# Alternating softmax and stick-breaking head groups, with two groups' attention in progress at once

## The chip, the cores and the metric

The kernel runs on one core of one Trainium2 chip. The metric is the time of one execution on the device, in microseconds: 2751.64 us, the median of three runs (2748.37 to 2760.12). The core's engines are TensorE (PE), VectorE (DVE), ScalarE (ACT), GpSimd (POOL) and SyncE (SP, which issues most DMAs). Each works through its own instructions in a fixed order; semaphores make one engine wait for another.

## What is computed

One layer of a residual block over 2048 positions of width 1024. The mixer has two kinds of attention side by side, then an output projection and a SwiGLU feed-forward:

```python
u    = rms_norm(h, norm1_w)
proj = u @ w_in                       # [dq | dk | dv | sq | sk | sv]
# softmax kind: 4 heads, two maps per head (q and k normed)
logits = q @ k.T * scale + bias[t5_bucket]      # chunk-causal mask
p      = softmax(logits)
y_diff = rms_norm((p[:, :, 0] - lam * p[:, :, 1]) @ v)
# stick-breaking kind: 8 heads, strictly causal, no softmax
z    = q @ k.T * scale
rem  = reverse_cumsum(log_sigmoid(-z)) - log_sigmoid(-z)
y_sb = rms_norm(exp(log_sigmoid(z) + rem) @ v)
h    = h + concat(y_diff, y_sb) @ w_out
u2   = rms_norm(h, norm2_w)
h    = h + (silu(u2 @ w_gate) * (u2 @ w_up)) @ w_down
```

All products keep close to float32 accuracy by splitting each operand into a high and a low fp16 part and adding three products.

## The kernel before, in words

**Groups.** The columns of `w_in` are cut into eight groups of 384 columns: groups 0 to 3 are one softmax head each (two maps of 64, values of 128), groups 4 to 7 are two stick-breaking heads each. For each group there is a projection (`proj`, 16 row tiles of 128 positions) and an attention (`diff_attn` or `sb_attn`, 16 query rows of 128).

**Softmax row** (`probs`). PE writes scores into PSUM (`sc`, up to 512 keys at a time). DVE copies each chunk to an SBUF buffer z with scale, bias and a running maximum (lines 483 and 487). DVE reduces the maxima into `ng` (line 492), ACT turns them into a bias (493) and takes Exp over the row with sums (497), at most four pieces: two maps by two blocks of 1024 keys. DVE then reduces the sums (500), takes a reciprocal and a factor (502, 503) and combines the two maps (507).

**Stick-breaking step** (`stage_a`), one head and one block of up to 1024 keys. For each chunk PE writes scores, ACT takes two sigmoids (554 into the buffer, 555 in place), DVE runs a scan along the keys (557) and a product (558).

**Values.** Either result is split into fp16 parts: a cast (line 89 on ACT or 93 on POOL) and a subtraction (98, mostly POOL). A transposing DMA turns it into `aT`, and PE multiplies with v into a PSUM buffer `yp` (458). After four rows (two rows in the last group) `finish` norms and splits the output: squares on ACT (416 or 418), a power on POOL (428 or 151), a product on DVE (429), transposes on PE, and the split into `mo` (435, 436), which goes to DRAM.

**Buffers.** The score buffers z (tag `z4`) are nine for both kinds: a softmax row beyond 1024 keys holds four, a stick-breaking step two. `sc` has four PSUM buffers, `yp` two, `aT` five, the fp16 split three.

**Order.** Groups are emitted one after another: 0 to 3, then 4 to 7. The projection runs half a group or more ahead (`advance`). A scheduler at build time then sets every engine's order from what is emitted, by priority, when operands and buffers are ready; the functions marked `pri("at")` have a priority of their own. In `sb_attn` a step's value products are put off by PD = 5 steps (`pend`), in `diff_attn` by one row.

**End of attention.** During the last half of group 7, output-projection rows (`out_proj`, line 761, evictions 764) are emitted between its steps as they become ready; `post` norms and splits each row for the feed-forward, which starts when the rest is done.

Of the kernel before, what the change touches and what calls it, by code (L numbers as in the profile page):

```python
# [11 lines left out]
F32 = mybir.dt.float32  # L12
# [26 lines left out]
QB, KB, ZB, AB, SB, PD = 4, 7, 9, 5, 3, 5  # L39
# [20 lines left out]
def block(tc, a, out):  # L60
# [3 lines left out]
    with top:  # L64
# [186 lines left out]
        with ExitStack() as ph1:  # L251
# [96 lines left out]
            def proj_batch(g, G, B):  # L348
# [3 lines left out]
                if g < 4:  # L352
                    rq = raw[:].rearrange("p t (c e) -> p t c e", e=64)
                    sq = st[:].rearrange("p c t s e -> p (c t s e)")[:, :2048].bitcast(F32)
# [24 lines left out]
            def proj(g, G, fresh=None):  # L379
                for t in range(NT):  # L380
# [6 lines left out]
                    if t % 4 == 0:  # L387
                        st = pp.tile([P, 6, 4, 2, 64], F16, tag="st", name=nm("st"))
                        v = sp.tile([P, 4, 256], F16, tag="v", bufs=KB, name=nm("v"))
                        raw = pp.tile([P, 4, 256], F32, tag="raw", name=nm("raw")) if g < 4 else None  # L390
# [68 lines left out]

            def diff_attn(g, G):  # L460
# [54 lines left out]
                def values(i, aTs, ssum):  # L515
                    r, k = fq(g, i)
                    if r == 0:
                        ypd[0] = ps.tile([P, 512], F32, tag="yp", name=nm("yp"))
                    yp = ypd[0]
                    for q, (b, n, aT) in enumerate(aTs):  # L520
                        pv(G, yp, P * r, aT, b, n, 0, 128, r == 0 and q == 0, r == k - 1 and q == len(aTs) - 1)
                    if r == k - 1:
                        finish(g, G, i, k, yp, ssum)

                prev = None
                for i in range(NT):
                    if i % 4 == 0:
                        level()
                    z = probs(i)
                    if prev is not None:  # L530
                        values(*prev)
                    yield ((i + 1) * (i + 2) / 2 + CD * (i + 1)) / (136 + 16 * CD), i + 1
                    prev = (i, z, sums[0])
                values(*prev)

            def sb_attn(g, G):
# [38 lines left out]
                pend = []  # L575
# [12 lines left out]
                for u in pend:  # L588
                    stage_b(*u)

# [101 lines left out]
            def proj_stream():  # L692
                for g in range(NG):
                    for t, _ in enumerate(proj(g, Gs[g], fresh if g == 0 else None)):
                        if g == 0 and t == 0:
                            build_bias()
                        if g == NG - 1 and t in WT:
                            if t == WT[0]:
                                rp2.extend(norm_gain(a["norm2_w"], w2))
                            load_wo(WT.index(t))  # L700
                        if t == PF and g + 1 < NG:
                            Gs[g + 1] = load_w(g + 1)
# [41 lines left out]
            def out_proj():  # L744
                for t in range(NT):
# [5 lines left out]
                    else:  # L751
                        xf = pp.tile([P, 6, 4, 2, 64], F16, tag="st", name=nm("xf"))[:].rearrange("p c t s e -> p (c t s e)").bitcast(F32)[:, :D]
# [38 lines left out]
            advance(NT - LAG0)  # L791
            for g in range(NG):
                advance(NT * g + 4)
                for fr, i in (diff_attn if g < 4 else sb_attn)(g, Gs[g]):
                    advance(max(NT * g + min(4 * (i // 4 + 1), NT), int(NT * (g + 1 + fr) - (LAG * (1 - LF * fr * (g == NG - 1)) if g else LAG0 + (LAG - LAG0) * fr))))
                    while g == NG - 1 and len(wos) == 4 and outs < Gs[g].get("fin", 0) and (outs + 2) * (outs + 3) / 272 < fr - LO:
                        next(op)
                        outs += 1
            while outs < 12:
# [428 lines left out]
```

## Time and profile before

| | us |
|---|---|
| median of three runs | 2751.64 |
| profiled execution | 2752.86 |
| its span | 2751.1 |
| first softmax Exp / last | 107.3 / 618.3 |
| first stick-breaking sigmoid / last | 612.7 / 1394.1 |
| first output-projection matmul / last | 1216.6 / 1470.9 |
| busy over the span: PE, DVE, POOL, ACT | 2489.3, 1967.9, 1428.8, 1357.8 |

The page's groups name a line of the kernel, an engine, and out<-in by the program's names. Busy time is the time in which at least one of the group's instructions runs; the idle time behind it is what the engine spent just before them, with what ended it. Matmul durations overlap, so the busy time over the count is the better price for one matmul.

### The profile page before, as it was taken

What the parts mean: (1) busy time and instruction counts of PE and PEld (TensorE: products, weight loads), DVE (VectorE), ACT (ScalarE), POOL (GpSimd) and SP (SyncE); (2) the same over time, 40 slices, a digit from 0 to 9 for tenths busy, and PEclk for the clock granted to TensorE, in tenths of its full rate; (3) what the DMA queues carried; (4) which work ended last, traced back from release to release, by engine and by line L of the source; (5) the groups of instructions that cost most, each with busy time, mean ns of one, the idle gap of its engine ahead of it and who ended that gap; (6) DMA issues with size and microseconds to landing.
All of it is one profiled execution on the core that took longest, in us unless ns stands there. A gap on an engine that the chain in (4) does not pass through costs nothing.

```text
span 2751.1 us, 45381 instructions
## 1 busy us (share of the span) xinstructions
PE 2489.3 (90%) x17084; PEld 1411.3 (51%) x17084; DVE 1967.9 (72%) x3752; ACT 1357.8 (49%) x2539; POOL 1428.8 (52%) x1002
## 2 busy tenths in 40 slices
PE   7998989898878786788988899999999999999999
PEld 4655555555545453457775444444444444444444
DVE  6888879797989989977655878777776644443434
ACT  4665656566878778765644535353342211121120
POOL 2567767665454545546655656555654322232322
PEclk9999999999999997989999999999999999999999
DMA  7788787879999988987887665656657845535532
GB/s 231 197 163 182 151 191 160 180 167 206 196 209 194 199 177 150 205 186 202 211 247 271 235 232 192 225 204 213 237 200 280 339 150 187 210 131 199 188 118 93
DMA packets 646829, 543.52 MB, mean 198 GB/s; under 512 B 506368, under 2 KB 573952, under 8 KB 636368
## 3 DMA queue, kind: packets, MB, share of 16 engines
q1 hardware_dynamic: 644784, 538.53, 71.7%
q8 instruction: 134, 2.20, 0.3%
q0 software_dynamic: 512, 1.36, 0.2%
q14 instruction: 87, 0.71, 0.1%
q10 hardware_dynamic: 1312, 0.72, 0.1%
HBM read 261.08 MB, written 147.32 MB: 148 GB/s over the span
## 4 chain that ended last, share of the span: by engine, by line
PE 33%; DVE 7%; DMA 6%; POOL 3%; issue 3%; ACT 2%; SPq 0%; DVEq 0%; POOLq 0%; ACTq 0%
PE pd L1034 12%; PE pm L934 7%; PE pd L934 6%; PE pa L934 5%; DVE wd L215 2%; DMA stages<-in_w_down_dram 1%; DMA aT<-s 1%; POOL stages L98 1%; PE po L761 1%; POOL s L98 1%; DMA X<-xcd 1%; DMA stages<-in_w_up_dram 1%; DVE wu L215 1%; DVE cg L98 1%; DVE cg L999 1%
## 5 line engine op out<-in xcount | busy, mean ns | idle before, releaser
L98 POOL TENSOR_TENSOR s<-z,s 128x1024 f16<-128x1024 f32 (+7 forms) x288 | 473.5, 1652 | 339.3 <-ACT s L89 300.5
L320 PE MATMUL pj<-w,xt 128*128 128x384 f16 x3072 | 574.4, 335 | 28.1 <-DVE st L330 12.6
L320 PEld LDWEIGHTS <-xt 128*128 128x128 f16 x3072 | 300.7, 100 | 239.6 <-issue 39.4
L448 PE MATMUL sc<-kT,qT 128*128 128x512 f16 (+3 forms) x1280 | 346.8, 361 | 72.8 <-DVE z L558 32.1
L557 DVE TENSOR_TENSOR_SCAN z<-z,sc 128x512 f32<-128x512 f32 (+3 forms) x320 | 355.5, 1113 | 70.7 <-ACT sc L555 68.5
L1034 PE MATMUL pd<-wd,act 128*128 128x512 f16 x1764 | 392.9, 380 | 8.5 <-DVE cu L968 7.0
L458 PE MATMUL yp<-v,aT 128*128 128x64 f16 (+1 forms) x4896 | 281.0, 208 | 79.1 <-DMA aT<-s 78.4
L458 PEld LDWEIGHTS <-aT 128*128 128x128 f16 x4896 | 244.9, 102 | 169.1 <-DMA aT<-s 107.7
L934 PEld LDWEIGHTS <-wg 128*128 128x128 f16 x1848 | 181.3, 98 | 224.4 <-issue 10.9
L934 PEld LDWEIGHTS <-wu 128*128 128x128 f16 x1848 | 181.7, 98 | 220.8 <-issue 8.2
L98 POOL TENSOR_TENSOR act<-cg,act 128x512 f16<-128x512 f32 x109 | 150.4, 1390 | 259.4 <-ACT act L993 259.4
L1034 PEld LDWEIGHTS <-act 128*128 128x128 f16 x1764 | 172.8, 98 | 217.0 <-issue 10.9
L89 ACT CAST s<-z 128x384 f16<-128x384 f32 (+7 forms) x216 | 170.5, 790 | 157.8 <-DMA aT<-s 65.4
L98 POOL TENSOR_TENSOR stages<-stages 128x512 f32<-128x512 f32 x97 | 170.2, 1755 | 120.2 <-DVE wg L215 43.2
L98 POOL TENSOR_TENSOR hs<-hs,cu 128x512 f32<-128x512 f32 x102 | 132.6, 1306 | 162.0 <-DVE hs L1040 60.2
L554 ACT ACTIVATE z<-sc,c 128x512 f32<-128x512 f32 (+3 forms) x320 | 203.5, 636 | 10.7 <-PE sc L448 5.9
L558 DVE TENSOR_TENSOR z<-sc,z 128x512 f32<-128x512 f32 (+3 forms) x320 | 193.3, 606 | 8.1
L555 ACT ACTIVATE sc<-sc,c 128x512 f32<-128x512 f32 (+3 forms) x320 | 195.7, 611 | 0.0
L761 PE MATMUL po<-wo,mt 128*128 128x256 f16 x1536 | 182.4, 277 | 11.4 <-DVE xf L764 6.8
L993 ACT CAST act<-cg 128x512 f16<-128x512 f32 x126 | 76.8, 616 | 231.3 <-DVE cg L999 193.4
L1040 DVE SCALAR_TENSOR_TENSOR hs<-pd,c,hs 128x512 f32<-128x512 f32 x144 | 106.2, 747 | 116.8 <-PE pd L1034 104.5
L934 PE MATMUL pm<-X,wu 128*128 128x512 f16 x792 | 179.3, 379 | 1.8 <-ACT cg L979 1.7
(241 smaller groups left out, 4109.9 us busy)
## 6 DMA issues: line engine op xcount, KB each, us to landing
xt<-xs SPq DMA_DIRECT2D x112, 512.0 KB, 4.3
hs<-hd SPq DMA_DIRECT2D x72, 512.0 KB, 4.4
hd<-hs SPq DMA_DIRECT2D x56, 512.0 KB, 6.1
split<-wg SPq DMA_DIRECT2D x11, 1792.0 KB, 6.9
split<-wu SPq DMA_DIRECT2D x11, 1792.0 KB, 6.7
split<-wd SPq DMA_DIRECT2D x11, 1792.0 KB, 6.8
wg<-split SPq DMA_DIRECT2D x11, 1792.0 KB, 7.4
wd<-split SPq DMA_DIRECT2D x11, 1792.0 KB, 9.1
```

Source lines behind the costliest of these rows:

```text
L89: ACT.copy(dst, src)
L98: (DVE if e == "D" else POOL).tensor_tensor(dst, a_, b_, op)
L320: PE.matmul(pj[:, :384], lhsT=xv[:, xi, kt, :], rhs=G["w"][:, wi, kt, :], start=n == 0, stop=n == 23)
L448: PE.matmul(sc[:, : 128 * w].rearrange("p (t n) -> p t n", n=P), lhsT=G["q"][i // 4][:, 2 - 2 * o + m, i % 4, :], rhs=G["k"][q][:, m, 0:w, ...
L458: PE.matmul(yp[:, y0 : y0 + wd], lhsT=aT[:, a_, :], rhs=v[:, v_ : v_ + wd], start=start and j == 0 and q == 0, stop=stop and j == nb - 1 a ...
L554: ACT.activation(om[:, lo:hi], sc[:, :w], AF.Sigmoid, scale=G["nkz"][:])
L555: ACT.activation(sc[:, :w], sc[:, :w], AF.Sigmoid, scale=G["kz"][:])
L557: DVE.tensor_tensor_scan(ov, ov, sc[:, :w], om[:, hi : hi + 1], op0=ALU.mult, op1=ALU.bypass)
L558: DVE.tensor_tensor(be[:, lo:hi], sc[:, :w], om[:, lo + 1 : hi + 1], ALU.mult)
L761: PE.matmul(po[:, sl], lhsT=mt[:, kt, P * xi : P * xi + P], rhs=wos[2 * h + n][wi][:, kt, :], start=q == 0, stop=q == 23)
L934: PE.matmul(ps_[:].rearrange("p (t n) -> p t n", n=P), lhsT=wv[:, wo, wi, 128 * kt : 128 * kt + 128], rhs=X[xo][:, :, xi, kt, :], start=st ...
L1034: PE.matmul(po[:], lhsT=act[:, ao, xi, 128 * j : 128 * j + 128], rhs=W["d"][:, wo, wi, :], start=start and u == 0 and q == 0, stop=u == nu ...
```

## The change

Groups are taken in the order 0, 4, 1, 5, 2, 6, 3, 7, for the projection as for the attention. A driver keeps up to two groups' attention alive. Each has a position: its place in the order plus twice the finished share of its work, so a group spans two units and its neighbour starts when it is half done. The driver always steps the group whose position is lowest. Value products of both kinds go through one list `pend`, put off by PD = 4 units. The projection's pace follows the position. Buffers for kT go from 7 to 8, for v from 7 to 9, and the projection's staging tile `st` shrinks from 6 to 4 parts. The norm2 gain, which lies in the tile of the softmax bias, is fetched once the last softmax group has ended. Output-projection rows start only when group 3 has ended, and a row needs both group 3 and group 7; how many may be out follows a line in the position instead of a square law.

```diff
-QB, KB, ZB, AB, SB, PD = 4, 7, 9, 5, 3, 5
+QB, KB, VB, ZB, AB, SB, PD = 4, 8, 9, 9, 5, 3, 4
+ORDER = (0, 4, 1, 5, 2, 6, 3, 7)
...
+            pend = []
+
+            def push(f):
+                pend.append(f)
+                while len(pend) > PD:
+                    pend.pop(0)()
...
-                    z = probs(i)
-                    if prev is not None:
-                        values(*prev)
+                    aTs = probs(i)
+                    for q, (b, n, aT) in enumerate(aTs):
+                        push(functools.partial(values, i, q, len(aTs), b, n, aT, sums[0]))
...
-                            pend.append((i, m, b, n, aT))
-                            if len(pend) > PD:
-                                stage_b(*pend.pop(0))
+                            push(functools.partial(stage_b, i, m, b, n, aT))
...
-            advance(NT - LAG0)
-            for g in range(NG):
-                advance(NT * g + 4)
-                for fr, i in (diff_attn if g < 4 else sb_attn)(g, Gs[g]):
-                    advance(max(NT * g + min(4 * (i // 4 + 1), NT), int(NT * (g + 1 + fr) - (LAG * (1 - LF * fr * (g == NG - 1)) if g else LAG0 + (LAG - LAG0) * fr))))
-                    while g == NG - 1 and len(wos) == 4 and outs < Gs[g].get("fin", 0) and (outs + 2) * (outs + 3) / 272 < fr - LO:
+            live, nxt = {}, 0
+            while live or nxt < NG:
+                if nxt < NG and all(v >= nxt for v, _ in live.values()):
+                    g = ORDER[nxt]
+                    live[nxt] = (nxt, (diff_attn if g < 4 else sb_attn)(g, Gs[g]))
+                    advance(NT * nxt + 4)
+                    nxt += 1
+                p = min(live, key=lambda k: live[k][0])
+                fr, i = next(live[p][1], (None, None))
+                if fr is None:
+                    del live[p]
+                    if p == NG - 2:
+                        while pend:
+                            pend.pop(0)()
+                        rp2.extend(norm_gain(a["norm2_w"], w2))
+                    continue
+                v = p + 2 * fr
+                live[p] = (v, live[p][1])
+                advance(max(NT * p + min(4 * (i // 4 + 1), NT), int(NT * v + LAG)))
+                if p == NG - 1 and p - 1 not in live and len(wos) == 4:
+                    done = min(Gs[g].get("fin", 0) for g in (3, 7))
+                    while outs < min(done, 12) and (outs + 2) / 14 < v - NG + LO:
                         next(op)
                         outs += 1
```

**The middle of a softmax row.** The row of 1408 keys (pieces of 1024 and 384). Before, on DVE, from the maxima's reduction (L492) to the sums' reduction (L500):

```order
L492 TENSOR_REDUCE ng_5325<-mx_5294 128x2
L503 TENSOR_SCALAR rc_5221<-rc_5221,c_261,sums_5049 128x1
L483 TENSOR_SCALAR z_5458,mx_5457<-sc_5463,c_230 128x512
L426 SCALAR_TENSOR_TENSOR yrs_5135<-yss_5130,er_5136 128x4
L507 SCALAR_TENSOR_TENSOR z_5184<-z_5198,rc_5221,z_5184 128x1024
L507 SCALAR_TENSOR_TENSOR z_5193<-z_5207,rc_5221,z_5193 128x256
L483 TENSOR_SCALAR z_5467,mx_5457<-sc_5468,c_230 128x256
L487 ISA z_5467,mx_5457<-sc_5468,bias,c_230 128x256
L487 ISA mx_5457 128x1
L483 TENSOR_SCALAR z_5473,mx_5457<-sc_5474,c_230 128x512
L429 TENSOR_TENSOR y_5129<-yp_4846,yrs_5135 128x512
L483 TENSOR_SCALAR z_5473,mx_5457<-sc_5478,c_230 128x512
```

The fill is the row before (5184) and the row after (5458); on ACT the bias is followed at once by the four Exps. In the change, DVE has these rows from the reduction (now L500) to the sums (now L508; scan L563, product L564):

```order
L500 TENSOR_REDUCE ng_10294<-mx_10263 128x2
L563 SCALAR_TENSOR_TENSOR z_10417<-z_10417,sc_10419 128x512
L564 TENSOR_TENSOR z_10416<-sc_10419,z_10417 128x512
L563 SCALAR_TENSOR_TENSOR z_10417<-z_10417,sc_10426 128x512
L564 TENSOR_TENSOR z_10416<-sc_10426,z_10417 128x512
L553 COPY z_10463<-z_10186 128x1
L508 TENSOR_REDUCE sums_9667<-s_10297 128x2
L510 RECIPROCAL rc_10303<-sums_9667 128x1
L511 TENSOR_SCALAR rc_10303<-rc_10303,c_261,sums_9667 128x1
```

and ACT has these, from the bias (now L501) on:

```order
L501 ACTIVATE ng_10294<-ng_10294,c_260 128x2
L560 ACTIVATE z_10417<-sc_10426,c_4361 128x512
L561 ACTIVATE sc_10426<-sc_10426,c_4360 128x512
L90 CAST s_10203<-z_10185 128x1024
L505 ACT_TABLE_LOAD
L505 ACTIVATE z_10264,s_10297<-z_10264,ng_10294 128x1024
L505 ACTIVATE z_10273,s_10297<-z_10273,ng_10294 128x384
L505 ACTIVATE z_10279,s_10297<-z_10279,ng_10294 128x1024
L505 ACTIVATE z_10288,s_10297<-z_10288,ng_10294 128x384
L560 ACT_TABLE_LOAD
L560 ACTIVATE z_10463<-sc_10465,c_4361 128x512
```

The neighbouring softmax rows have gone from DVE's fill and stick-breaking work has come; on ACT a chunk's sigmoids, a cast and a table load have come between the bias and the Exps.

**The end of the attention**, on DVE. Before, among the last scans (L557), products (L558) and the output projection's evictions (L764):

```order
L557 SCALAR_TENSOR_TENSOR z_18407<-z_18407,sc_18416 128x512
L545 MEMSET z_18453 128x1
L558 TENSOR_TENSOR z_18406<-sc_18416,z_18407 128x512
L557 SCALAR_TENSOR_TENSOR z_18453<-z_18453,sc_18455 128x512
L98 TENSOR_TENSOR x_18358<-z_18345,x_18358 128x2x512
L764 SCALAR_TENSOR_TENSOR xf_18776<-po_18778,c_14910,xf_18776 128x256
L558 TENSOR_TENSOR z_18452<-sc_18455,z_18453 128x512
L545 MEMSET z_18641 128x1
L557 SCALAR_TENSOR_TENSOR z_18453<-z_18453,sc_18463 128x512
L150 TENSOR_SCALAR xrs_18624<-xss_18622 128x1
L764 SCALAR_TENSOR_TENSOR xf_18776<-po_18829,c_15745,xf_18776 128x256
```

In the change, at the same distance from the end:

```order
L563 SCALAR_TENSOR_TENSOR z_18931<-z_18931,sc_18933 128x512
L564 TENSOR_TENSOR z_18930<-sc_18933,z_18931 128x512
L553 COPY z_18977<-z_18890 128x1
L563 SCALAR_TENSOR_TENSOR z_18931<-z_18931,sc_18940 128x512
L564 TENSOR_TENSOR z_18930<-sc_18940,z_18931 128x512
L563 SCALAR_TENSOR_TENSOR z_18977<-z_18977,sc_18979 128x512
L564 TENSOR_TENSOR z_18976<-sc_18979,z_18977 128x512
L563 SCALAR_TENSOR_TENSOR z_18977<-z_18977,sc_18986 128x512
L551 MEMSET z_19037 128x1
L564 TENSOR_TENSOR z_18976<-sc_18986,z_18977 128x512
```

Scans and products follow each other, and the evictions (now L762) of the output projection stand ahead of all of them or behind.

More of the change, by code (lines that the diff above doesn't have):

```diff
@@ L513, in diff_attn, with values @@
                 ypd = {}
-                def values(i, aTs, ssum):
+                def values(i, q, nq_, b, n, aT, ssum):
                     r, k = fq(g, i)
-                    if r == 0:
+                    if r == 0 and q == 0:
                         ypd[0] = ps.tile([P, 512], F32, tag="yp", name=nm("yp"))
                     yp = ypd[0]
[L520 to L525, printed above, removed]
+                    pv(G, yp, P * r, aT, b, n, 0, 128, r == 0 and q == 0, r == k - 1 and q == nq_ - 1)
+                    if q == nq_ - 1:
+                        if r == k - 1:
+                            finish(g, G, i, k, yp, ssum)
+                            G["fin"] = i + 1
                 for i in range(NT):
```

29 lines of the change are left out of this document (12 added, 17 removed).

## The prediction

> **What bounds the kernel now.** I read the windows of busy time first, to see which engine carries which stretch.
>
> ```profile
> core 0: us, PE busy (x) PEld busy (x) DVE busy (x) ACT busy (x) POOL busy (x), PEclk, DMA share, GB/s
> ...
> 100.00:620.00 520.00, 471.99 (x3734) 302.17 (x3731) 442.79 (x1324) 316.48 (x814) 358.24 (x255) 0.97 0.81 173
> 620.00:1200.00 580.00, 462.83 (x4710) 289.87 (x4709) 514.52 (x919) 449.12 (x868) 300.24 (x194) 0.92 0.95 191
> 100.00:1200.00 1100.00, 934.82 (x8442) 592.04 (x8440) 957.31 (x2242) 765.59 (x1681) 658.48 (x449) 0.94 0.88 183
> 1216.00:1471.00 255.00, 229.52 (x2356) 194.76 (x2355) 168.93 (x273) 135.65 (x215) 152.10 (x101) 0.97 0.85 234
> ...
> 1000.00:1100.00 100.00, 72.48 (x753) 44.38 (x750) 94.41 (x154) 84.37 (x155) 53.12 (x33) 0.83 0.91 170
> ```
>
> From 100 to 620 us the four softmax groups run: PE 472 of 520 (91%), DVE 443 (85%), ACT 316 (61%). From 620 to 1200 us it is the stick-breaking groups: DVE 515 of 580 (89%), ACT 449 (77%), PE 463 (80%). The two kinds lean on different engines, and that is the room the change can use: over the 1100 us the fullest engine is DVE with 957, so 143 us are idle on it. The row of 1000 to 1100 shows that DVE can run at 94%. From 1216 to 1471 us PE leads (230 of 255), because the output projection lies beside the last group. After 1471 us comes the feed-forward, whose code and order the change leaves alone; it only starts earlier or later.
>
> Then the waits of DVE between 100 and 1200 us (total, times, longest), since its idle time is what is for sale.
>
> ```profile
> DVE z L557 <- ACT sc L555: 36.9, 44, 2.9
> DVE z L483 <- PE sc L448: 17.7, 20, 2.1
> DVE y L429 <- POOL yrs L428: 17.7, 7, 5.4
> DVE v L330 <- ACT v L327: 16.5, 12, 3.8
> DVE yrs L426 <- ACT y L416: 8.0, 3, 5.7
> DVE ss L358 <- ACT st L355: 6.6, 6, 2.0
> DVE sums L500 <- ACT z L497: 5.9, 8, 1.6
> DVE mo L436 <- ACT mo L435: 3.6, 3, 2.1
> ```
>
> The seventh row is the one to remember: a softmax row's reduction of the exponentials' sums waited only 5.9 us in all for ACT.
>
> **The change part by part.**
>
> *Amount of work.* The order of instructions has the same matmuls and, within a few rows, the same DVE instructions as before; some 25 casts of the splits move from ACT to POOL. POOL has 1100 - 658 = 442 us idle beside them: no cost. If that cover were gone, a POOL subtraction of 2.2 us (row below) would be late, and the transposed weights behind it.
>
> *Table loads.* ACT now switches between Exp and Sigmoid inside each pair of groups: 97 loads in its order against 5. One costs this:
>
> ```profile
> L554 ACT ACT_TABLE_LOAD x2 | 2.6, 1283 | 0.0
> ...
> 611.43 1.28 ACT L554 ACT_TABLE_LOAD   x1
> 612.72 0.37 ACT L554 ACTIVATE z<-sc,c 128x128 f32<-128x128 f32 x1
> ```
>
> 92 more by 1.283 us are 118 us of ACT. ACT has 1100 - 766 = 334 us idle there and would go to 884 of 1100 (80%), so the sum itself hides. What does not hide is the load that lies in a chain DVE waits for, which is counted next.
>
> *The middle of a softmax row.* DVE reduces the row's maxima (ng), ACT takes the bias and up to four Exp, then DVE needs their sums. While ACT works, DVE lives on what stands in its own order between the two. The durations:
>
> ```profile
> L493 ACT ACTIVATE ng<-ng,c 128x2 f32<-128x2 f32 x56 | 16.4, 294 | 33.8 <-DVE ng L492 33.3
> L497 ACT ACTIVATE z<-z,ng 128x1024 f32<-128x1024 f32 x80 | 91.2, 1140 | 1.3
> L497 ACT ACTIVATE z<-z,ng 128x384 f32<-128x384 f32 x16 | 9.6, 603 | 0.2
> L554 ACT ACTIVATE z<-sc,c 128x512 f32<-128x512 f32 x224 | 157.0, 701 | 5.3 <-PE sc L448 3.6 <-issue 1.6
> L555 ACT ACTIVATE sc<-sc,c 128x512 f32<-128x512 f32 x224 | 151.7, 677 | 0.0
> L89 ACT CAST s<-z 128x1024 f16<-128x1024 f32 x83 | 87.1, 1050 | 77.6 <-issue 16.8 <-DMA xcd<-x 13.8 <-DVE z L558 12.2
> L557 DVE TENSOR_TENSOR_SCAN z<-z,sc 128x512 f32<-128x512 f32 x224 | 285.0, 1272 | 40.1 <-ACT sc L555 39.0 <-PE sc L450 0.4
> L558 DVE TENSOR_TENSOR z<-sc,z 128x512 f32<-128x512 f32 x224 | 153.3, 686 | 5.6
> L547 DVE COPY z<-z 128x1 f32<-128x1 f32 x64 | 9.1, 142 | 0.0
> ```
>
> Take the row of 1408 keys that the change section shows. Before, ACT needs 0.29 + 2 x 1.14 + 2 x 0.60 = 3.8 us, and DVE has about 7.4 us of the neighbouring softmax rows in between. In the change, a chunk's two sigmoids (0.70 + 0.68), a cast (1.05) and a table load (1.28) stand between the bias and the Exps, so ACT needs 7.5 us; DVE has two scans, two products and a copy, 2 x 1.27 + 2 x 0.69 + 0.14 = 4.1 us. DVE falls short by 3.4 us. Counted in the same way, each row of the order by the mean of its shape, over the 56 softmax rows that have such a reduction: before, ACT 3.3 and DVE 5.2 us on average, short in 4 rows, 4 us in all; in the change ACT 5.3 and DVE 4.1, short in 35 rows, 96 us in all. For before the profile has 5.9 us where the count says 4, so I trust the count. Added: 96.4 - 3.9 = **92.5 us**. What is late next is the split of that row (cast, subtraction, transposing DMA) and the next row's evictions, because the nine score buffers z are shared: a late softmax row holds four of them.
>
> The bounds of this term: not below 0, since the waits may fall where PE is the one that is late (PE is 85% busy); not above 92.5 by much, since ACT with 80% load is mostly there when DVE reduces.
>
> *The waits the second group can cover.* Of the quoted waits, those inside a softmax row, a group's finish or the projection's evictions (17.7 + 17.7 + 16.5 + 8.0 + 6.6 + 3.6 = 70.1 us) are answers that take a few us and for which a second stream can supply work. The scan's wait for ACT (36.9) I leave, as ACT gets fuller. Bounds: nothing covered (0), or the whole 143 - 6 = 137. I take **-70.1**.
>
> *The tail.* Output-projection rows now wait until both the last softmax group (3) and the last stick-breaking group (7) have the row, and are then issued in a burst. In DVE's order the last 20 scan chunks stand without a row of the output projection among them; before, they were mixed to the end.
>
> ```profile
> L448 PE MATMUL sc<-kT,qT 128*128 128x512 f16 (+3 forms) x108 | 29.7, 373 | 4.1 <-DVE z L545 1.5 <-DMA qT<-qT 1.2 <-DVE z L547 0.7
> L458 PE MATMUL yp<-v,aT 128*128 128x64 f16 x648 | 28.1, 195 | 11.0 <-DMA aT<-s 11.0
> L98 POOL TENSOR_TENSOR s<-z,s 128x1024 f16<-128x1024 f32 x120 | 263.5, 2199 | 162.6 <-ACT s L89 147.5 <-issue 9.0 <-DMA aT<-s 2.3
> ...
> DMA to landing us min/median/max: 2.3/4.4/7.8
> ```
>
> DVE needs about 38 us for the 20 chunks (1.27 + 0.69 each, two of them smaller). PE has in that place 40 score matmuls at 29.7/108 = 0.28 and 294 value matmuls at 28.1/648 = 0.043, with the mask some 25 us: 13 idle. Behind the last product a cast (1.05), a subtraction (2.2) and a transposing DMA (4.4) stand with nothing beside them: 8 more. **+21 us**; bounds 0 (PE still had stalls of 25 us between 1216 and 1471 that the burst may spare) and 40.
>
> *Edits with one answer.* More buffers for kT and v, a smaller st, one fewer pending unit, the norm2 gain fetched after group 3: no instruction more; SP's number of issues differs by one, and the two kinds' transposes average out DMA shares of 0.81 and 0.95. The gain's DMA goes behind group 3's last use of the bias tile, and only the first output row's normalization could wait for it, by the 4 to 8 us of a DMA landing, hidden under that row's projection.
>
> **Sum**, against the profiled execution's 2752.9 us (1.8 around its span of 2751.1, and 1.2 above the median of 2751.64): 2752.9 + 92.5 - 70.1 + 21 = **2796 us**, 1.6% slower.
>
> **The page on table loads.** The trace's load takes 1.28 us, and the next ACTIVATE starts 0.01 us after it. The Trainium skill, ScalarE: Activation LUTs, section "What ACT_TABLE_LOAD costs", gives about 1283 ns and a drain of about 1380 ns besides, 2.66 us for every switch. By that page 92 switches would be 245 us of ACT, and the 46 new loads ahead of Exps would lengthen the rows' chains by 46 x 1.38 = 63 us, an estimate from the page: 2859. The trace has the page's load but no drain behind it. The same page, section "Table sets: the hidden batching unit", says to group activations by set before switching, which is what the change gives up.
>
> **Rivals.**
>
> *Faster: PE becomes the bound.* DVE's 143 us of idle time could take up the short rows, and with two streams PE would always find a score or a projection to do. At the 91% that it has in the softmax part, 935 us take 1027, DVE then at 957/1027 = 93%, which the row of 1000 to 1100 us shows to be possible: 73 less, 21 more in the tail, 2701. For it: the engines' loads really are complementary. Against: a full DVE leaves no room for 35 short rows.
>
> *No change.* Half of the short rows fall where DVE waited anyway: 2752.9 + 46 - 70 + 21 = 2750.
>
> *Much slower: the shared yp buffers.* Both groups accumulate in one pool of two PSUM buffers, which one group had to itself. A finish holds its buffer through squares, power, product, transposes and the split. The profile's waits of 17.7, 8.0 and 3.6 us lie in it. If each of the 28 finishes between 100 and 1200 us stops the value products for about 3 us, five aT buffers fill and both streams stand: 84 more, 2880. It decides if PE's waits for the finish (yp on mo) exceed those for aT.
>
> *The switch costs more than the load.* If ACT had to empty its pipeline as well, by another 1.28 us, 46 x 1.28 = 59 us would come on top: 2855. The two quoted rows, back to back, speak against it.
>
> That the change doesn't interleave can be left out: the order alternates Exp and Sigmoid 46 times.
>
> **How the numbers follow.** The forecast has 0.45, faster 0.28, no change 0.15, yp 0.09, costlier switches 0.03. The forecast's own range is 2765 to 2850 (tail 0 to 40, covered waits 100 to 30). Reaching toward the faster case and the yp case gives **2690 to 2870** for 8 in 10. A measurement of this kernel tells about 0.5% (14 us) from no change. Faster: 0.28 and a little of the no-change case, 0.30. Same: 0.17. Slower: 0.53.
>
> **What would show it.** Right: DVE's wait at the sums' reduction (5.9 us before) grows to 60 us or more, ACT shows about 97 table loads at 1.28 us without gaps behind them, and DVE's busy share from 100 us to the first output-projection row falls below 87%. The tail: PE idle 20 us more between the first and the last output-projection row. Wrong: if that share rises to 90% or more, the short rows were hidden; if PE's largest wait is yp for mo, the shared buffers decide.

## The result, and the profile after

The changed kernel takes **2989.41 us** (median of four runs, 2978.88 to 2994.32) where the kernel before takes 2750.74 on the same chip: a ratio of 1.0856, 95% interval 1.0817 to 1.0895. It is 239 us slower; 44 were forecast, and the time lies outside the range of 2690 to 2870. The feed-forward from the last output-projection matmul to the end is unchanged: 2989.2 - 1710.5 = 1278.7 us of span after, 2751.1 - 1470.9 = 1280.2 before. All the loss lies ahead of it. The first output-projection matmul starts at 1391.1 instead of 1216.6 us (174.5 later), and the stretch to the last one takes 319.4 instead of 254.3 (65 more).

The line numbers of the attention move by 1 to 8 in the changed kernel: the sums' reduction is 508 (500 before), the scan 563 (557), the eviction of softmax scores 491 (483), of v 331 (330), the value products 459 (458).

Windows of busy time, changed kernel. The first is the stretch from 100 us to the first output-projection matmul, the second the stretch of the output projection, the third 20 us in the middle:

```profile
core 0: us, PE busy (x) PEld busy (x) DVE busy (x) ACT busy (x) POOL busy (x), PEclk, DMA share, GB/s
100.00:1391.00 1291.00, 1002.78 (x8503) 617.14 (x8501) 968.10 (x2236) 869.53 (x1751) 671.06 (x479) 0.89 0.75 161
1391.00:1711.00 320.00, 260.07 (x2527) 211.95 (x2524) 198.27 (x337) 165.58 (x267) 161.18 (x108) 0.89 0.73 199
740.00:760.00 20.00, 16.27 (x160) 10.63 (x157) 3.84 (x14) 6.75 (x23) 10.57 (x9) 1.00 0.83 166
...
0.00:100.00 100.00, 59.25 (x309) 36.63 (x310) 50.21 (x132) 37.30 (x77) 23.61 (x39) 0.83 0.52 163
```

DVE now has 968 of 1291 (75%, 87% before), PE 78% (85%), ACT 67% (70%): no engine became the bound, all three became emptier. Already the first 100 us hold less work: DVE 50 us, 70 in the row of before below. The third row is a seam, where one group ends and the next begins: DVE is busy for 3.8 of 20 us.

The same view, kernel before, for the first stretch:

```profile
0.00:100.00 100.00, 77.65 (x426) 48.63 (x427) 69.88 (x156) 48.03 (x97) 39.27 (x48) 0.97 0.68 218
```

DVE's waits in the changed kernel between 100 and 1450 us (total, times, longest), which answer to the eight rows of the prediction:

```profile
DVE sums L508 <- ACT z L505: 83.2, 27, 5.9
DVE z L563 <- ACT sc L561: 79.8, 67, 3.6
DVE v L331 <- ACT v L328: 32.4, 16, 6.2
DVE z L491 <- PE sc L449: 24.3, 22, 3.7
DVE rc L510 <- ACT z L505: 21.5, 16, 2.6
DVE yrs L427 <- ACT y L417: 13.2, 5, 4.4
DVE y L430 <- POOL yrs L429: 11.9, 4, 5.9
...
DVE mo L437 <- ACT mo L436: 4.6, 5, 1.8
```

The sums' wait is there, 83.2 + 21.5 = 104.7 us with the reciprocal behind it (5.9 + 0.7 before). But the waits that the second group was to cover have not gone: v 32.4 (16.5), scores 24.3 (17.7), yrs 13.2 (8.0).

The scan's wait for ACT is 79.8 here, where the prediction left it at 36.9; but that row ended at 1200 us, with part of the last group still to come. Over the whole execution, before (first line) and after (second), it is

```profile
DVE z L557 <- ACT sc L555: 68.5, 58, 6.8
DVE z L563 <- ACT sc L561: 106.8, 76, 7.7
```

so it grew by 38 us.

One of those softmax rows, first on ACT, then on DVE (start, duration, then what the engine waited for in brackets):

```profile
868.97 0.55 ACT L561 ACTIVATE sc<-sc,c 128x384 f32<-128x384 f32 x1
869.44 0.29 ACT L501 ACTIVATE ng<-ng,c 128x2 f32<-128x2 f32 x1
869.75 1.28 ACT L505 ACT_TABLE_LOAD   x1
871.04 1.15 ACT L505 ACTIVATE z<-z,ng 128x1024 f32<-128x1024 f32 x1
...
874.21 1.28 ACT L560 ACT_TABLE_LOAD   x1
875.50 0.69 ACT L560 ACTIVATE z<-sc,c 128x512 f32<-128x512 f32 x1
```

```profile
869.09 0.16 DVE L500 TENSOR_REDUCE ng<-mx 128x2 f32<-128x8 f32 x1
869.55 1.01 DVE L563 TENSOR_TENSOR_SCAN z<-z,sc 128x384 f32<-128x384 f32 x1 [0.30 <-ACT sc L561]
870.67 0.56 DVE L564 TENSOR_TENSOR z<-sc,z 128x384 f32<-128x384 f32 x1
871.14 0.14 DVE L553 COPY z<-z 128x1 f32<-128x1 f32 x1
874.22 0.16 DVE L508 TENSOR_REDUCE sums<-s 128x2 f32<-128x4 f32 x1 [2.93 <-ACT z L505]
```

Between the maxima and the sums DVE has one scan, one product and a copy, then 2.93 us of nothing: the short row of the forecast. Each load takes 1.28 us and the next ACTIVATE starts 0.01 us behind it. The groups of loads, changed kernel (busy us, mean ns, idle before):

```profile
L560 ACT ACT_TABLE_LOAD x48 | 61.6, 1283 | 0.8
L505 ACT ACT_TABLE_LOAD x47 | 60.3, 1283 | 0.8
```

PE's waits, 100 to 1450 us, changed kernel. The buffers `yp`, the heaviest rival, are in the last row with 4.5 us:

```profile
PE sc L449 <- DVE z L564: 66.5, 44, 5.2
PE yp L459 <- DMA aT<-s: 65.9, 49, 6.2
PE sc L449 <- DVE z L551: 44.7, 14, 7.5
...
PE yp L459 <- DVE mo L437: 4.5, 4, 1.2
```

So about 100 us of waiting are where the prediction put them. A wait is not yet lost time, and 239 us were lost; the experiments look for where.

### The profile page after: what moved, and what is told of

It is laid out like the page before. It is cut to its first block, busy times and chain, and to the rows that moved or that the text cites. A ratio compares the mean times of both kernels' runs of the same rounds, so it can differ in the third digit from the quotient of the medians.

```text
span 2989.2 us, 45476 instructions
## 1 busy us (share of the span) xinstructions
PE 2555.6 (85%) x17084; PEld 1432.6 (48%) x17084; DVE 1973.7 (66%) x3752; ACT 1464.0 (49%) x2607; POOL 1431.3 (48%) x1026
## 4 chain that ended last, share of the span: by engine, by line
PE 34%; DVE 9%; DMA 7%; ACT 5%; issue 4%; POOL 3%; SPq 0%; DVEq 0%; ACTq 0%; POOLq 0%
PE pd L1050 11%; PE pm L950 7%; PE pd L950 5%; PE pa L950 5%; PE po L759 2%; DVE wd L216 2%; DMA aT<-s 2%; DMA stages<-in_w_down_dram 1%; DVE z L563 1%; PE pj L321 1%; POOL s L99 1%; ACT z L505 1%; DVE wu L216 1%; POOL stages L99 1%; DMA stages<-in_w_up_dram 1%
## 5 line engine op out<-in xcount | busy, mean ns | idle before, releaser
L321 PE MATMUL pj<-w,xt 128*128 128x384 f16 x3072 | 596.2, 346 | 39.7 <-ACT raw L342 15.9
L99 POOL TENSOR_TENSOR s<-z,s 128x1024 f16<-128x1024 f32 (+7 forms) x288 | 462.1, 1617 | 244.1 <-ACT s L90 241.1
L449 PE MATMUL sc<-kT,qT 128*128 128x512 f16 (+3 forms) x1280 | 358.3, 379 | 185.7 <-DVE z L564 75.4
L321 PEld LDWEIGHTS <-xt 128*128 128x128 f16 x3072 | 310.1, 103 | 275.8 <-issue 90.0
L563 DVE TENSOR_TENSOR_SCAN z<-z,sc 128x512 f32<-128x512 f32 (+3 forms) x320 | 354.8, 1113 | 111.4 <-ACT sc L561 106.8
L94 POOL TENSOR_SCALAR s<-z 128x1024 f16<-128x1024 f32 (+7 forms) x89 | 86.5, 978 | 370.7 <-DVE z L515 327.3
L449 PEld LDWEIGHTS <-qT 128*128 128x128 f16 x1280 | 109.6, 102 | 279.9 <-DVE z L564 87.0
L90 ACT CAST s<-z 128x1024 f16<-128x1024 f32 (+7 forms) x199 | 155.8, 789 | 171.6 <-DMA aT<-s 115.3
L560 ACT ACTIVATE z<-sc,c 128x512 f32<-128x512 f32 (+3 forms) x320 | 204.3, 638 | 56.9 <-PE sc L449 27.8
L564 DVE TENSOR_TENSOR z<-sc,z 128x512 f32<-128x512 f32 (+3 forms) x320 | 192.1, 605 | 7.1
L561 ACT ACTIVATE sc<-sc,c 128x512 f32<-128x512 f32 (+3 forms) x320 | 196.5, 614 | 0.0
```

What stands on the lines that cost most here:

```text
L90: ACT.copy(dst, src)
L99: (DVE if e == "D" else POOL).tensor_tensor(dst, a_, b_, op)
L321: PE.matmul(pj[:, :384], lhsT=xv[:, xi, kt, :], rhs=G["w"][:, wi, kt, :], start=n == 0, stop=n == 23)
L449: PE.matmul(sc[:, : 128 * w].rearrange("p (t n) -> p t n", n=P), lhsT=G["q"][i // 4][:, 2 - 2 * o + m, i % 4, :], rhs=G["k"][q][:, m, 0:w, ...
L560: ACT.activation(om[:, lo:hi], sc[:, :w], AF.Sigmoid, scale=G["nkz"][:])
L561: ACT.activation(sc[:, :w], sc[:, :w], AF.Sigmoid, scale=G["kz"][:])
```

## The experiments

All times are medians beside the kernel before on the same chip (2749 to 2752 us); ratios are to it, with the 95% interval.

### What do the table loads cost?

`e_tanh`: both sigmoids become Tanh, which the kernel can take without switching from Exp (2 loads in the trace instead of 97). It computes another function; the shapes and the order are the change's.

```diff
-ACT.activation(om[:, lo:hi], sc[:, :w], AF.Sigmoid, scale=G["nkz"][:])
-ACT.activation(sc[:, :w], sc[:, :w], AF.Sigmoid, scale=G["kz"][:])
+ACT.activation(om[:, lo:hi], sc[:, :w], AF.Tanh, scale=G["nkz"][:])
+ACT.activation(sc[:, :w], sc[:, :w], AF.Tanh, scale=G["kz"][:])
```

> The changed kernel with Tanh in place of both Sigmoids of the stick-breaking step, so that Exp and this function lie in one table: the order of ACT then holds 2 table loads instead of 97. It leaves out the right values (its output is not the reference's); every instruction's shape and cost stays. Theory loads (the switches are what the change pays): 46 loads ahead of Exps and as many ahead of sigmoids go, 59 to 118 us less than 2989, so 2870 to 2930, and DVE's wait at the sums' reduction falls from 105 to 50 us. Rival buffers and order (two groups in one set of buffers make the engines wait whatever the table): less than 30 us gained, above 2960.

2936.23, ratio 1.0662 [1.0644, 1.0679]: the 95 loads, 121.9 us of ACT, cost 53 us of time. DVE's waits (same view as above) tell where:

```profile
DVE sums L508 <- ACT z L505: 52.4, 25, 4.6
DVE z L563 <- ACT sc L561: 49.5, 44, 3.7
...
DVE rc L510 <- ACT z L505: 8.7, 8, 2.1
```

That is 31 us less waiting at the sums, 13 less at the reciprocal and 30 less at the scan (29 over the whole execution, 106.8 to 77.9). So the loads ahead of the sigmoids are waited for as well as those ahead of the Exps; the prediction counted only the latter. The gain lies a little short of the forecast 59 to 118, and well above the rival's 30. 52 us of the sums' wait remain without the loads; what the order shown ahead of the prediction still has there is the other kind's two functions per chunk and a cast.

### Alternating kinds, or two groups in progress?

`e_same` keeps two groups in progress but takes them in the old order (15 loads). `e_one` keeps the new order but finishes each group before the next.

```diff
 e_same
-ORDER = (0, 4, 1, 5, 2, 6, 3, 7)
+ORDER = (0, 1, 2, 3, 4, 5, 6, 7)
 e_one
-if nxt < NG and all(v >= nxt for v, _ in live.values()):
+if nxt < NG and not live:
```

> The changed kernel with the groups in the old order 0 to 7, two in progress as in the change: the two streams are then of one kind, but where group 3 meets group 4. 15 table loads. Theory loads: nearly all of the loss goes, 2760 to 2840. Rival buffers: two streams still share nine z, five aT and two yp, so the loss stays, 2900 to 3000.

> The changed kernel with the groups alternating but only one in progress (the next starts when the one before has ended): 17 table loads, new projection pace and new end as in the change. Theory loads and rival buffers both: the interleaving was the cost, so 2750 to 2830. Rival head and tail (the dropped advance of the first projection and the burst of output rows cost more than the interleaving): above 2850.

`e_same` 2866.22, 1.0413 [1.0395, 1.043]; `e_one` 2815.18, 1.0223 [1.0206, 1.024]. `e_same` falls between its two expectations: it is 123 faster than the change, more than the 53 of the loads. Against the alternating order without loads (2936) it is 70 faster, so at these buffer sizes and with this head, alternating costs more than its loads. `e_one` is in its forecast range. Having two groups in progress costs 2989 - 2815 = 174 us with alternating kinds, the extra loads included. The remaining 64 (2815 against 2751) belong to the edits around the interleaving. In `e_one`'s DVE waits (100 to 1450 us) the sums are back at 15 us and v at 11; the scan's wait for ACT, 75.4, is all that this execution has of it, 31 under the change's:

```profile
DVE z L563 <- ACT sc L561: 75.4, 65, 5.5
DVE sums L508 <- ACT z L505: 15.1, 7, 4.9
...
DVE v L331 <- ACT v L328: 11.0, 9, 4.0
```

### The head

Before, the driver began with `advance(NT - LAG0)`: the whole projection of group 0 (16 row tiles, as `LAG0` is 0) was emitted ahead of its first attention row. The new driver has no such line.

```diff
 e_head, x_one_head
+            advance(NT - LAG0)
             live, nxt = {}, 0
 b_nohead (from the kernel before)
-            advance(NT - LAG0)
...
-... (LAG * (1 - LF * fr * (g == NG - 1)) if g else LAG0 + (LAG - LAG0) * fr) ...
+... LAG * (1 - LF * fr * (g == NG - 1)) ...
```

> The changed kernel with the whole projection of group 0 emitted ahead of its attention again, as before the change. In the first 300 us the changed kernel's DVE is 80 us behind the same amount of busy time before, PE 55 us. Rival head: 50 to 80 us less, 2910 to 2940. Theory loads: the head is only early work done late, less than 20 us, above 2970.

> The changed kernel with both undone: one group in progress at a time (groups still alternating), and the projection of group 0 emitted ahead of its attention. If the two act apart, 2815 - 47 = 2768; what is left above 2751 is then the new end, the new projection pace and the alternation itself. If the late head only cost because two groups followed it, it stays near 2815.

> The kernel before, with one part of the change alone: the projection of group 0 is not emitted ahead of its attention any more (the advance by 16 row tiles dropped, the later pace as for the other groups). Theory head: the same 47 us that its return gave in the changed kernel, 2790 to 2805. Rival: with one group in progress the scheduler fills the gap, below 2765.

`e_head` 2942.4 (1.0691 [1.0675, 1.0707]): 47 less than the change and just above the forecast 2910 to 2940. Its first 100 us are as full as before (windows of `e_head`):

```profile
0.00:100.00 100.00, 74.47 (x420) 47.36 (x421) 69.23 (x158) 47.91 (x97) 39.26 (x48) 0.95 0.68 218
```

One group at a time and the head (`x_one_head`) gives 2771.4 (1.0068 [1.0043, 1.0093]), 44 less than without. `b_nohead` takes the head away from the kernel before: 2853.19, 1.0385 [1.0368, 1.0403], 104 more. That is outside both its expectations. There it also drops the slower pace of group 0, so 104 is not a second measure of the same 47, but of the sign there is no doubt. One deleted line, which no sentence of the prediction names, is a fifth of the loss.

### The buffers

A group has four kT tiles. With two groups in progress the older holds its four to its end while the younger fills its own, and with eight in all the third group's tiles have to wait for the seam. The window of 740 to 760 us above is a seam; DVE there (`v` from the projection, the older group's finish, then the first row of the next group):

```profile
744.57 0.49 DVE L331 SCALAR_TENSOR_TENSOR v<-pj,v 128x128 f16<-128x128 f32 x2 [2.07 <-ACT v L328]
750.96 0.69 DVE L430 TENSOR_TENSOR y<-yp,yrs 128x512 f32<-128x512 f32 x1 [5.90 <-POOL yrs L429]
753.70 0.29 DVE L331 SCALAR_TENSOR_TENSOR v<-pj,v 128x128 f16<-128x128 f32 x1 [2.05 <-ACT v L328]
755.80 0.75 DVE L437 SCALAR_TENSOR_TENSOR mo<-yp,c,mo 128x512 f16<-128x512 f32 x1 [1.80 <-ACT mo L436]
758.59 0.35 DVE L495 CUSTOM_DVE_ANT_0 z<-sc,bias,c 128x128 f32<-128x128 f32 x1 [2.04 <-PE sc L449]
```

and PE, which has idled 0.81 us for the new group's own kT before its first scores (the transposing DMA into kT starts at 751.95 us, after POOL's subtractions for that batch's `st`, from 747.67 on):

```profile
755.99 0.49 PE L449 MATMUL sc<-kT,qT 128*128 128x128 f16 x4 [0.81 <-DMA kT<-st]
```

The trace shows the batch late; it does not show an instruction waiting for a free tile, since the order was fixed at build time. Whether the number of tiles is the reason, the sizes must tell. Four kernels change sizes alone (kT, v, z; the change has 8, 9, 9):

```diff
-QB, KB, VB, ZB, AB, SB, PD = 4, 8, 9, 9, 5, 3, 4
+QB, KB, VB, ZB, AB, SB, PD = 4, 7, 7, 9, 5, 3, 4     # x_kv
+QB, KB, VB, ZB, AB, SB, PD = 4, 7, 7, 10, 5, 3, 4    # x_zb10
+QB, KB, VB, ZB, AB, SB, PD = 4, 8, 9, 8, 5, 3, 4     # x_zb8
+QB, KB, VB, ZB, AB, SB, PD = 4, 9, 10, 8, 5, 3, 4    # x_kb9
```

> The changed kernel with the buffers for kT and v at 7 each, as before the change (the change has 8 and 9). It is the reference for the next kernel. Two groups hold eight kT while both are complete, but they are half a group apart: 0 to 30 us slower, 2985 to 3020.

> As the kernel with 7 buffers for kT and v, and with ten score buffers z in place of nine, in the room that these leave. Theory buffers: nine z for a softmax row (4) and two or three stick-breaking steps (2 each) are what both streams wait for, so 30 to 80 us less than the kernel with 7 and 9. Rival: the wait is in the order of ACT and DVE, less than 10 us between the two.

> The changed kernel with eight score buffers z in place of nine; the reference for the next kernel. Ten in place of nine brought 22 us where kT and v had 7 each. Theory buffers z: 30 to 80 us slower, 3020 to 3070. If z hardly matters: 2990 to 3010.

> As the kernel with eight z, and with nine buffers for kT and ten for v (8 and 9 in the change), in the room of that z. With 7 and 7 the change lost 150 us more, and where a group ends (740 to 758, 1098 to 1112 us of its trace) DVE is idle for some 15 us until the next group's first kT lands. Theory kT: the first batch of the next group but one then needs no group to end first: 30 to 80 us less than the kernel with eight z. Rival: at 8 and 9 the two groups fit, within 10 us.

| kT, v, z | us | ratio |
|---|---|---|
| 7, 7, 9 | 3138.62 | 1.1415 [1.1391, 1.1439] |
| 7, 7, 10 | 3116.69 | 1.1334 [1.1311, 1.1356] |
| 8, 9, 9 (the change) | 2989.41 | 1.0856 [1.0817, 1.0895] |
| 8, 9, 8 | 2995.59 | 1.0901 [1.0884, 1.0917] |
| 9, 10, 8 | 2946.74 | 1.0728 [1.0711, 1.0745] |

From the sizes of the kernel before, the change's own kT and v buffers are worth 149 us (0 to 30 were expected), and one more of each another 49 at eight z (2996 to 2947; 43 against the change itself). kT and v were not varied apart, so which of the two is short stays open. The shared z, nine for two kinds, matter little: 6 for one less, which is within the intervals, and 22 for one more where kT and v are short. In `x_kb9` the emptiest 20 us between 100 and 1400 have 8.2 us of DVE (3.8 in the change), and five such stretches are under 12 us (eight in the change, nineteen in `x_kv`, four in the kernel before), counted over all 65.

`x_late` lets the next group begin 0.15 units later, so that the older is nearer to its end.

```diff
-if nxt < NG and all(v >= nxt for v, _ in live.values()):
+if nxt < NG and all(v >= nxt + 0.15 * (nxt > 1) for v, _ in live.values()):
```

> The changed kernel, but from the third group on a group starts only when the one in progress is 0.15 of a unit (7.5% of its work) further than in the change, so that the freed kT buffers are filled in the meantime. Theory kT: 20 to 60 us less, 2930 to 2970. Rival: the gap only moves, since one group alone then runs for that stretch: 2980 to 3000.

2973.82, 1.0824 [1.0803, 1.0844]: 16 less by the medians, outside both expectations, and its interval overlaps that of the change (1.0817 to 1.0895). It decides nothing; a shorter overlap would gain on any of the other costs too.

### A theory that fell: POOL's queue

In the changed kernel POOL's casts of the softmax split wait for DVE's combination of the two maps, 254 us for the widest of them (groups by shape, changed kernel) and 327 for all widths:

```profile
L94 POOL TENSOR_SCALAR s<-z 128x1024 f16<-128x1024 f32 x40 | 55.1, 1379 | 283.6 <-DVE z L515 254.0 <-issue 20.3 <-DMA aT<-s 6.6
```

If the other group's subtractions stood behind them, taking these casts off POOL would help. `x_pool` puts them on ACT and DVE:

```diff
-aTs.append((b, n, split_t(z0[:, :n], n)))
+aTs.append((b, n, split_t(z0[:, :n], n, "AD")))
```

> The changed kernel with the softmax rows' split cast kept off POOL (ACT or DVE take it). In the changed kernel POOL waits 327 us in its order for the softmax combination before such a cast, and stick-breaking subtractions stand behind it. Theory queue: these are late through it, the aT weights with them, so 20 to 50 us less, 2940 to 2970. Theory buffers: POOL is not what ends last, within 10 us or somewhat slower for the fuller ACT and DVE, 2980 to 3010.

3015.37, 1.0953 [1.0925, 1.0981]: 26 slower, where 20 to 50 less were forecast. POOL's queue was not the price. A reason that fits is that ACT's time is not spare: it is busy for 921 us between 100 and 1391, 870 in the change.

### Do the parts add up?

`x_fix` has the head and 9, 10, 8 buffers; `x_fix_tanh` besides takes the loads out (Tanh, another function again); `x_fix_same` has the same repairs with the old order of groups.

```diff
 x_fix
-QB, KB, VB, ZB, AB, SB, PD = 4, 8, 9, 9, 5, 3, 4
+QB, KB, VB, ZB, AB, SB, PD = 4, 9, 10, 8, 5, 3, 4
...
+            advance(NT - LAG0)
 x_fix_tanh: the same, and Tanh for Sigmoid
 x_fix_same: the same as x_fix, and
-ORDER = (0, 4, 1, 5, 2, 6, 3, 7)
+ORDER = (0, 1, 2, 3, 4, 5, 6, 7)
```

> The changed kernel with two causes removed: the projection of group 0 ahead of its attention, and nine buffers for kT and ten for v (eight z). If the two add up: 2989 - 47 - 49 + 6 = 2900. If both were one lack (too little of the next group ready), 2930 or more.

> The kernel with the two causes removed and Tanh in place of both Sigmoids (the stick-breaking step computes another function at the same cost), so that the table loads go too. If all three add up: 2900 - 53 = 2847, so that some 95 us above the kernel before belong to something else. If the loads were what held the rest: below 2800.

> The kernel with the two causes removed and the groups in the old order, so that the two in progress are of one kind. Theory mixing (a softmax row's turn from DVE to ACT and back is no longer covered by the next softmax row): two of one kind lose only the end, 2765 to 2790. Rival two in progress (nine z, five aT and two yp are too few for any two groups): 2830 or more.

`x_fix` 2895.42 (1.0517 [1.049, 1.0545]): the two repairs add, 94 of 47 + 43 to 49. `x_fix_tanh` 2822.04 (1.0255 [1.0228, 1.0283]), 25 below the sum of the parts: with the two repairs the loads weigh 73, not 53; `x_fix` also has ten more of them (105 at L505, L560 and L561, where the change has 95). `x_fix_same` 2822.1 (1.0254 [1.0229, 1.028]), between its two expectations: the same time, though that the medians agree to a tenth of a microsecond is chance (both spread over 6 to 8 us). With the repairs and without the loads, mixing two kinds is neither better nor worse than two groups of one kind, though the kinds do load different engines. At the change's own sizes and with its late head mixing was 70 worse (2936 against 2866), because the two repairs together give 94 with alternating kinds and 44 with one kind (2866 to 2822). The waits do not add up to time either: sums and reciprocal wait 59.6 + 6.5 us in `x_fix_tanh` and 32.2 + 3.0 in `x_fix_same`.

### The tail, and the remainder

`x_one_tail` is `x_one_head` with the old square law for the number of output rows; `x_same_tail` does the same to `x_fix_same`. Both still need group 3 and group 7 for a row.

```diff
-while outs < min(done, 12) and (outs + 2) / 14 < v - NG + LO:
+while outs < min(done, 12) and (outs + 2) * (outs + 3) / 272 < fr - LO:
```

> One group at a time, alternating, with the first projection ahead (2771), and the old square law for how many output-projection rows may be out. Theory tail: the burst costs the 21 us that were forecast, so 2750. Rival (the pace of the projection and the order cost it): within 7 us of 2771.

> Old order, two groups of one kind in progress, 9 kT / 10 v / 8 z buffers, the head's advance restored, and now also the old square law for the output rows instead of the burst at the end. Without that last edit the same kernel took 2822. If the burst costs here what it cost with one group at a time (2771.4 to 2743.6), 28 less: 2794, and 43 over the kernel before remain for having two groups in progress. If the two-in-progress remainder lies mostly in the tail, 2765 or less. If it stays above 2810, the tail is no part of it.

`x_one_tail` **2743.61** (ten runs; 0.9979 [0.9965, 0.9993]), `x_same_tail` 2788.63 (1.0135 [1.0117, 1.0152]): the burst costs 28 with one group at a time and 33 with two. `x_one_tail` is the fastest kernel here, 0.2% under the one before: the alternating order, one group at a time, with the head and the square law as they were. It keeps the change's smaller `st`, its PD, its late norm2 gain and the rule that a row needs both last groups, so with one group at a time these cost nothing that can be measured. Its scan waits longer for ACT than that of the kernel before (68.5), and still it is not slower:

```profile
DVE z L563 <- ACT sc L561: 91.9, 70, 7.1
```

So that wait alone does not say how long a kernel takes. Its windows, against the prediction's rows of before (957 of 1100 for DVE, 935 for PE), show the same fill:

```profile
100.00:1200.00 1100.00, 945.96 (x8537) 602.79 (x8536) 957.22 (x2260) 778.89 (x1701) 668.32 (x463) 0.94 0.88 186
```

Between `x_one_tail` and `x_same_tail` 45 us are left with the head and the tail mended, more kT and v, and few loads (they differ in order and sizes as well). The same window of `x_same_tail`:

```profile
100.00:1200.00 1100.00, 922.86 (x8155) 579.57 (x8154) 933.17 (x2191) 740.82 (x1642) 649.01 (x439) 0.94 0.86 179
```

By 1200 us it has 24 us less of DVE's work behind it and 23 less of PE's, and its stretch of the output projection takes 303 us (1202.8 to 1505.5) against 268 (1190.1 to 1458.1). One candidate is the list of put-off value products, which two groups now share; each has half the lag. `x_pend5` gives it room:

```diff
 x_pend5 (from x_fix_same)
-QB, KB, VB, ZB, AB, SB, PD = 4, 9, 10, 8, 5, 3, 4
+QB, KB, VB, ZB, AB, SB, PD = 4, 9, 10, 7, 6, 3, 5
```

> The kernel of 2822 (old order, two of one kind, repaired buffers and head, burst at the end) with 5 pending units of value products instead of 4, 6 aT buffers instead of 5 and 7 z instead of 8 for the room. The queue of pending units is shared by the two groups in progress, so each has half the lag that one group alone had. If this lag is the remainder, PE's wait for aT in the value products (81 us there) falls by 30 or more and the time to 2795 or less. If it is not, 2815 to 2835 (one z less cost 6 at most in an earlier run).

2832.23 (1.0293 [1.0276, 1.031]), 10 slower, and PE's wait for `aT` did not fall (90.5 us, 81.2 in `x_fix_same`). So this gave no sign of the lag being the remainder; it does not rule it out, because the seven z were felt: DVE waits 18.5 us for POOL's split of a z before it writes scores there (L491 and L495), 2.8 in `x_fix_same`. What the remainder is stays open; other numbers of `sc` and `yp` buffers and other priorities of the scheduler were not tried.

## Why the prediction was right and wrong

**Direction: right, size wrong.** Slower had 0.53; the loss was more than five times the forecast.

**The steps that failed** are three terms of the sum: the covered waits, put at -70.1, where these waits grew by 16 to 18 and two groups in progress, with the other costs mended, were some 45 us slower than one; the "edits with one answer", put at nothing, where one more buffer each for kT and v gave 43 to 49 us; and the removed head, which has no term and cost 47.

**The short softmax rows, +92.5: right in mechanism, place and size, as a wait.** The forecast had 5.9 + 92.5 = 98.4 us for the waits between the maxima and the combination of the maps; sums and reciprocal have 104.7. What this wait costs in time no run shows by itself. Less than half of it is the loads (31 us at the sums and 13 at the reciprocal, 21.5 against 8.7, fall away with Tanh, 44 of 104.7); what stays is there with the other kind's instructions in the same queue.

**Table loads: the price right, one half of their effect missed.** They are 1.283 us each, 97 in number, and back to back with their neighbours. The prediction let 118 us of ACT hide except ahead of Exps. The loads ahead of sigmoids make DVE's scan wait too (79.8 against 49.5 us without loads). Measured: 53, or 73 with head and buffers mended. The sentence "The scan's wait for ACT (36.9) I leave, as ACT gets fuller" was wrong as well: a fuller ACT was a reason to raise it, and over the whole execution it went from 68.5 to 106.8; 29 of these 38 us go when the loads go. What that is worth in time is not shown, since the fastest kernel has 91.9. The Trainium skill, ScalarE: Activation LUTs, section "What ACT_TABLE_LOAD costs", names about 1380 ns of drain besides each load; in the row shown the load starts 0.02 us after ACT's instruction before it, and the next starts 0.01 us after the load. Its section "Table sets: the hidden batching unit" says to batch by set, and the 53 to 73 us agree with that.

**The waits that the second group covers, -70.1: wrong.** v, scores, y, yrs, ss and mo waited 70.1 us before (72.3 if the window too ends 59 us after the first output-projection matmul) and 88.3 after (32.4 + 24.3 + 11.9 + 13.2 + 1.9 + 4.6); only y (17.7 to 11.9) and ss (6.6 to 1.9) became shorter. A reason that fits, though only a row at the sums was followed through the trace: a queue has one order, so a second group supplies work only where the order puts it between question and answer. With the repairs made and the loads taken out the two kinds gained nothing over two of one kind (2822 and 2822), and two groups lost against one (2789 and 2744). The same count that the prediction made for the sums, applied to these waits, was not made.

**"Edits with one answer": wrong.** "More buffers for kT and v ... no instruction more" is true and beside the point. The question was not what the added buffers cost but whether 8 and 9 are enough for two groups. One more of each: 49 us at eight z. Seven, as before, would have been 149 worse. No instruction count shows this. The likely mechanism, read from the kernel, is how long the older group holds its tiles, with the work that has to begin at the seam; the runs show only that the sizes matter.

**The head: missing.** The removed `advance(NT - LAG0)` stands in the diff, next to the new driver, and no term has it: 47 us.

**The tail, +21: right.** 28 and 33 measured for the burst (with one group at a time and with two of one kind), within its bounds of 0 to 40. PE's idle time between the first and the last output-projection matmul went from 25 to 60 us (+34, 20 forecast).

**The size.** 2989 - 2796 = 193. The head has 47 of it, the buffers 43 to 49, the credit that was not received 70, the tail 7 to 12. These overlap and are not a sum that has to close, and what is left is not assigned. By steps from the change downward: head 47, buffers 47, loads 73, two groups in progress 51, burst 28 (2989, 2942, 2895, 2822, 2771, 2744). The fourth step is not clean: the kernel of 2771 has the buffers of the change and 17 loads again. The forecast's own range of 2765 to 2850 is also narrower than the bounds it names, which together give 2745 to 2855.

**Rivals.** PE as the bound: PE fell to 78%. No change: 239 us slower. The yp buffers: PE waited 4.5 us for them, 65.9 for aT. Costlier switches: no gap at the loads. The signs that the prediction named all came out on its side (sums' wait at least 60, 97 loads without gaps, DVE share 75% under 87%, PE's idle time in the tail), and the time was still outside its range: none of the signs tested the covered waits or the terms put at nothing.

## What to carry to other kernels

When a change interleaves two streams on in-order engines, ask of every wait what the new order puts between question and answer on that engine; "a second stream can supply work" is not an answer. Count for how long the older stream holds each buffer and whether the next one can start before it lets go, and go through the diff's removed lines as carefully as through the added ones. Complementary averages of two stages say little: mixing the kinds here gained nothing even with the table loads taken out.

## What the runs showed of the hardware

The mean granted clock went with TensorE's busy share: 0.968 at 90% before, 0.932 at 85% in the change, 0.899 at 83% in `x_kv`, 0.967 at 90% in `x_one_tail`. The same 17084 matmul rows were busy for 2489.3, 2555.6, 2612.4 and 2477.1 us. So the change, which leaves TensorE waiting more, also has 66 us more of matmul time. That the gaps lower the clock was not tested apart, and not all of these 66 us need lie on the path that sets the time.

A table load takes 1.283 us with no gap around it in the trace. 95 of them cost 53 us of time, less than half of the 121.9 us that they keep ACT busy.
